# Rows of small factors spread over the partitions: through a scratch row in HBM instead of through TensorE

## The chip, the cores and the metric

The kernel runs on one core of one Trainium2 chip. The metric is the device time of one execution in microseconds (us). The kernel before was timed in three runs; the profile is of one further execution, taken by the hardware profiler.

The core has a matrix engine (TensorE, PE in the profile, with PEld for its weight loads), VectorE (DVE), ScalarE (ACT), GpSimd (POOL) and SyncE (SP). Each engine takes its own instructions in order. DMAs are issued from an engine's queue (here SP's for nearly all loads, POOL's for the ones that add to what is already there) and are moved by 16 DMA engines that all queues share. Work on different engines is ordered by semaphores. SBUF is the memory of 128 partitions that the engines work from, PSUM the one that TensorE writes, HBM the large one outside.

## The reference, cut to what matters

One layer of a decoder trunk, 512 tokens, 1024 channels, in float32:

```python
h = rmsnorm(x, norm1_g) * (1 + scale1) + shift1
qa, ka, va, qd, kd, vd, ga, gd = split(h @ w_in)
out_a = sliding_window_attention(qa, ka, va, sinks)
out_d = differential_attention(qd, kd, vd, lam)              # 4 heads of 128 channels
out_d = rmsnorm(out_d, subln_g) * (1 - lam_init)             # per head
merged = sigmoid(ga) * (out_a @ w_branch_swa) + sigmoid(gd) * (out_d @ w_branch_diff)
x = x + gate1 * (merged @ w_out)
h2 = rmsnorm(x, norm2_g) * (1 + scale2) + shift2
x = x + gate2 * conv_ffn(h2)                                 # up, conv, GELU * gate, down
return rmsnorm(x, final_g)
```

`shift`, `scale` and `gate` come from a small vector `c` by `silu(c) @ w_ada + b_ada`. Two kinds of small factors matter here. The norm of each differential head needs one reciprocal root per token (512 per head). `gate1` and `gate2` are one factor per channel (1024 each).

## The kernel before, in words

Products of two float32 matrices are made of three matmuls of parts (`mm3`, L107 to 110): each operand is split into a rounded high part (a cast on ScalarE) and the remainder (a subtraction on VectorE, `split`, L104).

The order of TensorE's work is written out by hand. The attention part is a list of score, transposition and value steps, with `fill(n)` between them: a fill takes n ticks, and in each tick one step (three matmuls) of a unit is done. Units are the projections that are left: of queries and keys (`add_q`, `add_head`), the two gates' projections with the branches' (`add_gate_a`, `add_gate_d`, `add_merge`). A unit's weights are loaded and split up to two units ahead; `recent` holds the last two subtractions of such splits. `after(n, fn)` calls `fn` n ticks later. VectorE's, ScalarE's and POOL's orders are in most stretches set by a planner, which takes what is ready by priority; `tc.high_priority` and `tc.issue_after` steer it.

Where the change is:

- **The heads' norm.** `diff_values(h)` (L705 to 736) multiplies the probabilities and the values of head h into a bank of PSUM, in which tokens lie along the row and the head's 128 channels over the partitions. ScalarE writes the squares `sq` and the scaled values `of`. After STAT_LAG ticks `stats` sums the squares by four small matmuls (L723), which leaves one sum per token, with the tokens over the partitions: a tile of 128 x 4. The root `rs` (tile `drs`) is made of it on VectorE and POOL (L134 to 151, the power on POOL at L141). But `of` has its tokens along the row, so each root is needed in all partitions of a column. `spread`, NORM_LAG ticks later, does that on TensorE: it broadcasts a column of `rs` to 128 x 128 and transposes it against the identity (L730), four times, into a bank of PSUM `rb`. VectorE multiplies `of` by it (L731), and the result is split into `vv`, the branch's operand in `add_merge`.
- **The gates.** The 32 columns of `late_mod` are filled by VectorE, one per load of a piece of `w_ada` (`ada_rows`, L754). Columns 0 to 7 are `gate1` (`g1c`), 24 to 31 `gate2` (`g2c`), with channels over the partitions. The weights of the output projection are multiplied by `gate1` along their rows (`load_rows`, L987), and the results of the down projection by `gate2` (L1613 and what calls it), so each needs all 1024 factors in every partition. `spread_rows` (L904) does it in two halves of four transpositions (L901) and a copy by ScalarE (L902): for `gate1` 12 ticks after its unit list begins (G1_AT), for `gate2` right before the output projection.
- **The first softmax of the sliding-window part** (L800 to 805): the softmax of head pair 0, then the remainders of two blocks of values (`keep_v(6, (1,))` and two more, L449) and of the second query tile (`stack(..., high=False)`, L426). `turn_va` transposes values into the bank that `keep_v(6, ...)` reads, so it has to wait for it (L486).

Of the kernel before, what the change touches and what calls it, by code (L numbers as in the profile page):

```python
# [8 lines left out]
F32 = mybir.dt.float32  # L9
# [5 lines left out]
P = 128  # L15
D = 1024
S = 512
KT = D // P
NT = S // P
# [6 lines left out]
DIFF_HEADS = 4  # L26
WB = 3
HP = 100000
ST = 6
ADA_LATE = 180  # L30
ADA_EVERY = 5
G1_AT = 12
STAT_LAG = 10
NORM_LAG = 16
VA_AT = 5
SWA_FILL = (2, 1, 6, 2, 2, 2, 2, 3)
DIFF_FILL = (3, 2, 4, 2)
# [6 lines left out]
def kernel(  # L44
# [19 lines left out]
    nc = tc.nc  # L64
# [3 lines left out]
    def pool(name, bufs=1, space=None, stack=ctx):  # L68
        kw = {} if space is None else {"space": space}
        return stack.enter_context(tc.tile_pool(name=name, bufs=bufs, reuse_waits="tile", **kw))  # L70

    cpool = pool("const")
    big = pool("big")
    wp = pool("w")
    ps = pool("ps", space=PSUM)

    def bank(tag, bufs, shape, name, dt=F32):
        return ps.tile(shape, dt, tag=tag, bufs=bufs, name=name)

    def fbank(name):  # L80
        return bank("f", 2, [P, S], name)

    def sbank(name, shape=(P, S)):
        return bank("s", 3, list(shape), name)

    def tbank(name, shape=(P, S)):
        return bank("t", 2, list(shape), name)

    def vbank(name):
        return bank("v", 1, [P, S], name)  # L90

    def raw_tile(shape, name):
        return wp.tile(shape, F32, tag="raw", bufs=4, name=name)

    casts, lows, recent = [None], [None], [None, None]

# [7 lines left out]
    def split(hi, lo, src):  # L104
        return nc.scalar.copy(hi, src), nc.vector.tensor_sub(lo, src, hi.bitcast(F32))

    def mm3(o, lh, ll, rh, rl, start, stop):  # L107
        nc.tensor.matmul(o, lh, rh, start=start, stop=False)  # L108
        nc.tensor.matmul(o, lh, rl, start=False, stop=False)  # L109
        nc.tensor.matmul(o, ll, rh, start=False, stop=stop)  # L110


    ident = cpool.tile([P, P], F32, name="ident")
# [53 lines left out]
    def rstd_m2(dst, ssq, n, d, wpool, plus=None):  # L167
        rstd_end(dst, *rstd_start(ssq, n, d, wpool, plus), n, wpool)
# [41 lines left out]
    acc = [sbank("aka"), sbank("aqa0"), sbank("aqa1"), fbank("av0"), fbank("av1"), vbank("ava"), tbank("av2"), tbank("av3")]  # L210
# [10 lines left out]
    qsc = cpool.tile([P, 4], F32, name="qsc")  # L221
# [153 lines left out]
    for k in range(KT):  # L375
        n = k + 1
# [24 lines left out]
    ap = pool("att", stack=at)  # L401
    qa = big.tile([P, 4, 2, S], F32R, tag="qa", name="qa")
# [15 lines left out]
    def stack(dst, src, scale, soon=True, high=True, low=True):  # L418
        with tc.high_priority(offset=HP) if soon else ExitStack():
            sc = [scale if isinstance(scale, float) else scale[own] for own, _ in halves]  # L420
            for j in range(2) if high else ():
                own = halves[j][0]
                nc.scalar.activation(dst[own, j], src[own], AF.Copy, scale=sc[j])
            for j in range(2) if low else ():
                own, other = halves[j]
                nc.vector.scalar_tensor_tensor(  # L426
                    dst[other, j], src[own], sc[j], dst[own, j].bitcast(F32), ALU.mult, ALU.subtract
                )
# [13 lines left out]
    def keep_v(i, parts=(0, 1)):  # L442
        t = TOKENS[i] * P
        hi, lo = (v[:, :, t : t + P] for v in vv)
        src = acc[i].rearrange("p (h d) -> p h d", d=P)
        if 0 in parts:
            nc.scalar.copy(hi, src)
        if 1 in parts:
            nc.vector.tensor_sub(lo, src, hi.bitcast(F32))  # L449
# [33 lines left out]
    def turn_va():  # L483
        pv = tbank("pva")
        for t in range(NT):
            nc.tensor.transpose(pv[:, t * P : (t + 1) * P], vaT[:, t * P : (t + 1) * P], ident)  # L486
        nc.scalar.copy(va.rearrange("p t d -> p (t d)"), pv)
# [42 lines left out]
    def after(n, fn):  # L530
        later.append([n, fn])
# [40 lines left out]
    def swa_softmax(i):  # L572
        with tc.high_priority(offset=HP):
            c = pairs[i]
            for j in range(2):
                h = i + 4 * j
                slope = 2.0 ** -(h + 1)
                nc.vector.tensor_scalar(c.nm[:, j], c.mx[:, j], -slope, nsink[:, h : h + 1], ALU.mult, ALU.min)
                nc.scalar.activation(c.es[:, j], c.nm[:, j], AF.Exp, bias=sink[:, h : h + 1])
                for n in range(NT):  # L580
                    w = P if n == 0 else 2 * P
                    nc.scalar.activation(
                        c.sb[n][:, j, :w], c.sb[n][:, j, :w], AF.Exp, bias=c.nm[:, j, n : n + 1], scale=slope,
                        accum_out=c.lsum[:, j, n : n + 1],
                    )
                nc.vector.tensor_add(c.lsum[:, j], c.lsum[:, j], c.es[:, j])
                nc.vector.reciprocal(c.lsum[:, j], c.lsum[:, j])
                for n in range(NT):
                    w = P if n == 0 else 2 * P
                    c.end = nc.vector.tensor_scalar_mul(c.sb[n][:, j, :w], c.sb[n][:, j, :w], c.lsum[:, j, n : n + 1])  # L590
# [114 lines left out]
    def diff_values(h):  # L705
        aTh, aTl = aTs[h]
        o = vbank(f"od{h}")
        for k in range(NT):
            q0 = k * P
            mm3(  # L710
                o[:, q0:], vv[0][:, h, k * P : (k + 1) * P], vv[1][:, h, k * P : (k + 1) * P],
                aTh[:, k * AW + q0 : k * AW + 512], aTl[:, k * AW + q0 : k * AW + 512],
                k == 0, k == NT - 1,
            )
        sq = big.tile([P, S], F32, tag="sq2", name=f"sq{h}")
        of = big.tile([P, S], F32, tag=("kvA", "kvB")[h % 2], name=f"of{h}")
        nc.scalar.activation(sq, o, AF.Square)
        nc.scalar.activation(of, o, AF.Copy, scale=sublnc)

        def stats():  # L720
            pss = tbank(f"pss{h}", (P, NT))
            for n in range(NT):
                nc.tensor.matmul(pss[:, n : n + 1], sq[:, n * P : (n + 1) * P], ones[:, 0:1], start=True, stop=True)  # L723
            rs = ap.tile([P, NT], F32, tag="drs", bufs=2, name=f"drs{h}")
            rstd_m2(rs, pss, NT, P, ap)

            def spread():
                rb = tbank(f"rb{h}")
                for n in range(NT):
                    nc.tensor.transpose(rb[:, n * P : (n + 1) * P], rs[:, n : n + 1].to_broadcast([P, P]), ident)  # L730
                nc.vector.tensor_mul(of, of, rb)  # L731
                split(vv[0][:, h], vv[1][:, h], of)

            after(NORM_LAG, spread)

        after(STAT_LAG, stats)


# [55 lines left out]
    with tc.issue_after(vat_copy.ins):  # L794
        fill(SWA_FILL[0])
        swa_scores(0, 0)
        with tc.issue_after(pairs[0].last.ins):
            fill(SWA_FILL[1])
            swa_scores(0, 2)
    with tc.issue_after(pairs[0].last.ins), tc.issue_after(vat_copy.ins):  # L800
        swa_softmax(0)
        keep_v(6, (1,))
        stack(qa[:, 1], acc[2], qsc[:, 1:2], high=False)
        keep_v(4, (1,))
        keep_v(7, (1,))

        lp = cpool.tile([P, 2, 64], F32, name="lp")
        ls = cpool.tile([P, 2], F32, name="ls")
        nlam = cpool.tile([P, 1], F32, name="nlam")
        nc.vector.tensor_mul(lp, lamv[:, 0:4:2], lamv[:, 1:4:2])  # L810
        nc.vector.reduce_sum(ls, lp, axis=mybir.AxisListType.X)
        nc.scalar.activation(ls, ls, AF.Exp)
        nc.vector.tensor_sub(nlam, ls[:, 1:2], ls[:, 0:1])
        nc.vector.tensor_scalar_add(nlam, nlam, -LAM_INIT)
        fill(VA_AT)
        turn_va()
        fill(SWA_FILL[2] - VA_AT)
# [28 lines left out]
    for s in range(4 * DIFF_HEADS):  # L846
        h, n = divmod(s, NT)
# [45 lines left out]
    g1b = gpart(4, [P, D], "g1b")  # L893
    g1c, s2c, a2c, g2c = (late_mod[:, 8 * i : 8 * i + 8] for i in range(4))
    nc.vector.tensor_add(g1c, g1c, blate[:, 0:8])
    nc.vector.tensor_scalar_mul(g1c, g1c, 0.5)

    def spread_half(dst, src, name, hf):
        pr = tbank(f"{name}{hf}")
        for k in range(4):  # L900
            nc.tensor.transpose(pr[:, k * P : (k + 1) * P], src[:, 4 * hf + k : 4 * hf + k + 1].to_broadcast([P, P]), ident)  # L901
        nc.scalar.copy(dst[:, hf * S : (hf + 1) * S], pr)  # L902

    def spread_rows(dst, src, name):  # L904
        for hf in range(2):
            spread_half(dst, src, name, hf)

    after(G1_AT, lambda: spread_rows(g1b, g1c, "pg1"))

    def add_gate_d(j):  # L910
        def gate(wts):
# [54 lines left out]
    nc.vector.scalar_tensor_tensor(a2c, a2c, 1.0, n2g, ALU.add, ALU.mult)  # L966
    nc.vector.tensor_scalar_mul(a2c, a2c, -0.5)
    g2row = big.tile([P, D], F32, tag="row", name="g2row")
    spread_rows(g2row, g2c, "pg2")
    g2b = [g2row[:, hf * S : (hf + 1) * S] for hf in range(2)]  # L970

    x1 = big.tile([P, NT, D], F32, tag="qa", name="x1")
# [318 lines left out]
    last = range(KT - TAIL, KT)  # L1291
# [541 lines left out]
```

## Time and profile before

| | us |
|---|---|
| median of 3 runs | 680.72 |
| lowest and highest run | 680.48, 680.81 |
| the profiled execution, its own time | 680.29 |
| its span in the profile | 678.4 |
| TensorE busy | 669.2 |
| VectorE busy | 569.2 |
| ScalarE busy | 402.2 |
| POOL busy | 66.0 |

Times in the profile count from the start of its span. The attention part runs from about 54 to 242 us, the merge of the branches to 296, the output projection and the norm to 350, the up-projection to 566, the down projection to the end. In the profile, a chain is the work that ended last, followed backwards; a piece of it is the time that a group of instructions adds to the end. In rows of instructions come start, duration, engine, line, operation, what is written and read, and the shape; in rows of groups the count, then the shortest, median and longest duration in ns, and the first and last start in us.

### The profile page before, as it was taken

The page shows a single profiled execution, that of the slowest core. Times are in us where ns is not written, and L with a number is a line of the kernel's source. Part 1 is how long each engine was busy: PE and PEld are TensorE (multiplying, and loading weights), DVE is VectorE, ACT ScalarE, POOL GpSimd, SP SyncE. Part 2 cuts the span into 40 slices and gives each one's busy share as a digit, 9 for nine tenths or more (in the row PEclk, how much of TensorE's full clock was granted, in tenths as well). Part 3 has the DMA queues.
Part 4 walks back from the last instruction along what each step waited for, and adds up shares of the span by engine and source line. Part 5 has one row for each costly group of instructions (what it writes and reads, how often), then busy time and mean ns, then how long its engine had stood idle before and what let it go on. Part 6 is the DMA issues. An engine that isn't in the chain of part 4 may idle for free.

```text
span 678.4 us, 10826 instructions
## 1 busy us (share of the span) xinstructions
PE 669.2 (99%) x4047; PEld 594.8 (88%) x4047; DVE 569.2 (84%) x1054; ACT 402.2 (59%) x702; POOL 66.0 (10%) x74
## 2 busy tenths in 40 slices
PE   8999999999999999999999999999999999999995
PEld 8888887888888888888899999999999998888885
DVE  6988987788887488973689998888888999979997
ACT  6678778565654233342597656565556566656665
POOL 2000000001000000000020120011111003440300
PEclk9999999999999999999999999999999999999999
DMA  9962131444354289767374988887876658996903
GB/s 357 418 227 65 63 125 63 138 143 154 82 168 156 93 291 309 262 173 244 116 126 109 224 211 202 195 201 167 216 172 182 144 187 193 196 205 189 165 0 125
DMA packets 71077, 119.68 MB, mean 176 GB/s; under 512 B 3952, under 2 KB 47728, under 8 KB 71024
## 3 DMA queue, kind: packets, MB, share of 16 engines
q1 hardware_dynamic: 52960, 95.04, 41.6%
q0 software_dynamic: 17776, 23.60, 21.5%
q8 instruction: 32, 0.52, 0.3%
q10 hardware_dynamic: 288, 0.34, 0.2%
q14 instruction: 21, 0.17, 0.1%
HBM read 116.87 MB, written 2.10 MB: 175 GB/s over the span
## 4 chain that ended last, share of the span: by engine, by line
PE 97%; DVE 1%; DMA 1%; ACT 0%; issue 0%; ACTq 0%
PE up L1159 33%; PE dc L1762 15%; PE av L351 3%; PE pga L108 2%; PE pga L110 2%; PE pga L109 2%; PE pgd L110 2%; PE oc L1215 2%; PE pgd L108 2%; PE oc L1216 2%; PE oc L1219 2%; PE pgd L109 2%; PE aqa L348 2%; PE sd L659 2%; PE pq L108 1%; PE pk L108 1%
## 5 line engine op out<-in xcount | busy, mean ns | idle before, releaser
L1159 PE MATMUL up<-t,m_whi 128*128 128x256 f32 x512 | 93.2, 283 | 0.0
L1159 PEld LDWEIGHTS up<-t,m_whi 128*128 128x128 f32 x512 | 79.9, 192 | 0.0
L1159 PE MATMUL up<-t,m_wlo 128*128 128x256 f32 x256 | 72.5, 284 | 0.0
L1159 PE MATMUL up<-bl,p_whi 128*128 128x256 f32 x232 | 65.8, 284 | 0.0
L1159 PE MATMUL up<-bh,p_wlo 128*128 128x256 f32 x232 | 65.8, 284 | 0.0
L1159 PE MATMUL up<-bh,p_whi 128*128 128x256 f32 x232 | 65.8, 284 | 0.0
L1159 PEld LDWEIGHTS up<-t,m_wlo 128*128 128x128 f32 x256 | 49.2, 192 | 0.0
L1159 PEld LDWEIGHTS up<-bh,p_wlo 128*128 128x128 f32 x232 | 44.6, 192 | 0.0
L1159 PEld LDWEIGHTS up<-bh,p_whi 128*128 128x128 f32 x232 | 44.6, 192 | 0.0
L1159 PEld LDWEIGHTS up<-bl,p_whi 128*128 128x128 f32 x232 | 44.6, 192 | 0.0
L1062 POOL DMA_DIRECT2D s<-in_w_up_dram x21 | 27.0, 1365 | 158.2 <-DMA s<-in_w_up_dram 116.8
L1090 ACT CAST m_whi<-s 128x1024 fp32r<-128x1024 f32 x31 | 32.4, 1046 | 15.7 <-DVE s L1084 9.1
L754 DVE CUSTOM_DVE_ANT_0 ra<-ra,csb 128x1024 f32<-128x1024 f32 x32 | 38.7, 1221 | 1.0 <-DMA ra<-in_w_ada_t_dram 1.0
L1094 DVE TENSOR_TENSOR m_wlo<-s,m_whi 128x1024 fp32r<-128x1024 f32 x31 | 37.9, 1221 | 1.3 <-ACT m_whi L1090 1.3
L1159 PE MATMUL up<-t,p_whi 128*128 128x256 f32 x176 | 32.2, 284 | 0.0
L684 ACT ACTIVATE sd<-sd,dmx 128x128 f32<-128x128 f32 (+3 forms) x32 | 17.8, 557 | 21.4 <-DVE dmx L682 17.1
L1159 PEld LDWEIGHTS up<-t,p_whi 128*128 128x128 f32 x176 | 27.5, 192 | 0.1
L1090 ACT CAST p_whi<-wa 128x1024 fp32r<-128x1024 f32 x18 | 18.8, 1042 | 12.6 <-PE up L1159 10.8
L141 POOL TENSOR_TENSOR r<-ms,mhalf 128x4 f32<-128x4 f32 x4 | 5.3, 1322 | 213.7 <-DVE ms L137 213.7
L1166 ACT ACTIVATE gT<-a,cols 128x512 f32<-128x512 f32 x22 | 17.6, 812 | 13.4 <-DVE a L1201 13.0
L1094 DVE TENSOR_TENSOR p_wlo<-wa,p_whi 128x1024 fp32r<-128x1024 f32 x18 | 22.0, 1224 | 4.0 <-ACT p_whi L1090 3.8
L1159 PE MATMUL up<-t,p_wlo 128*128 128x256 f32 x88 | 24.9, 283 | 0.0
(530 smaller groups left out, 2057.8 us busy)
## 6 DMA issues: line engine op xcount, KB each, us to landing
ra<-in_w_ada_t_dram SPq DMA_DIRECT2D x32, 512.0 KB, 4.0
wa<-in_w_up_dram SPq DMA_DIRECT2D x22, 512.0 KB, 4.1
s<-in_w_up_dram SPq DMA_DIRECT2D x21, 512.0 KB, 4.7
s<-in_w_up_dram POOLq DMA_DIRECT2D x21, 512.0 KB, 6.9
adaw<-in_w_ada_t_dram SPq DMA_DIRECT2D x15, 512.0 KB, 9.9
a<-in_w_up_dram SPq DMA_DIRECT2D x11, 512.0 KB, 4.9
b<-in_w_down_dram SPq DMA_DIRECT2D x10, 512.0 KB, 3.7
w<-in_w_first_dram SPq DMA_DIRECT2D x8, 512.0 KB, 9.9
```

The costliest lines, as they stand in the source:

```text
L108: nc.tensor.matmul(o, lh, rh, start=start, stop=False)
L109: nc.tensor.matmul(o, lh, rl, start=False, stop=False)
L110: nc.tensor.matmul(o, ll, rh, start=False, stop=stop)
L351: nc.tensor.matmul(acc[i], ht[:, t : t + P], wts[k][w][:, S:], start=start, stop=stop)
L684: nc.scalar.activation(pm[m], pm[m], AF.Exp, bias=mx[:, m : m + 1], scale=slope, accum_out=lsum[:, m : m + 1])
L754: nc.vector.tensor_tensor_reduce(r, r, csb, 1.0, 0.0, ALU.mult, ALU.add, late_mod[:, idx : idx + 1])
L1062: nc.gpsimd.dma_start(dst, upblock(*blk), accum_op=ALU.add)
L1090: nc.scalar.copy(W[J, name][0], R[J, SRC[name]])
L1094: nc.vector.tensor_sub(lo, R[J, SRC[name]], hi.bitcast(F32))
L1159: nc.tensor.matmul(o[u], w[:, k, cu], b[:, k], start=name in ("p1", "m5", "p2") and k == 0 and x == 0, stop=k == 3 and x == 2, skip_group_ ...
L1166: nc.scalar.activation(grow(j), av[J][:, u], AF.Identity, bias=cv[:, 66 + j : 67 + j], scale=cv[:, 44 + j : 45 + j])
L1762: nc.tensor.matmul((bank2[u] if o is None else o)[:, sl], a[:, q, cu], b[:, q, sl], start=first_mm and x == 0, stop=last_mm and x == 2, sk ...
```

## The change

`spread`'s and `spread_rows`' transpositions go. A new helper `to_rows` writes the small tile to a scratch row in HBM, in the order in which the factors are wanted, and reads that row back into all 128 partitions. Both DMAs are issued from POOL's queue, the second after the first has landed. The heads' rows land in a tile of SBUF instead of a bank of PSUM; the last head's takes the place of `sq`. The store is started right behind the root, in `stats`. STAT_LAG goes from 10 to 6 and NORM_LAG from 16 to 20, so that the product of `of` keeps its tick, and this product is now placed behind the subtractions in `recent`. The gates' rows are started as soon as the program reaches them. Besides, `keep_v(6, (1,))` gets high priority and stands ahead of the first softmax, and the `stack` behind it loses its own.

```diff
-G1_AT = 12
-STAT_LAG = 10
-NORM_LAG = 16
+STAT_LAG = 6
+NORM_LAG = 20
...
+    dp = pool("rows", space=bass.MemoryType.DRAM)
...
+    def to_rows(dst, src, n, name):
+        d = dp.tile([n, P], F32, name=name)
+        nc.gpsimd.dma_start(d.rearrange("k q -> q k"), src)
+        nc.gpsimd.dma_start(dst, d.rearrange("k q -> (k q)").partition_broadcast(P))
...
             rs = ap.tile([P, NT], F32, tag="drs", bufs=2, name=f"drs{h}")
             rstd_m2(rs, pss, NT, P, ap)
 
+            last = h == DIFF_HEADS - 1
+            rb = big.tile([P, S], F32, tag="sq2", name="rb3") if last else ap.tile([P, S], F32, tag="rb", name=f"rb{h}")
+            to_rows(rb, rs, NT, f"rs{h}")
+
             def spread():
-                rb = tbank(f"rb{h}")
-                for n in range(NT):
-                    nc.tensor.transpose(rb[:, n * P : (n + 1) * P], rs[:, n : n + 1].to_broadcast([P, P]), ident)
-                nc.vector.tensor_mul(of, of, rb)
+                with ExitStack() as place:
+                    for b in recent:
+                        place.enter_context(tc.issue_after(b.ins))
+                    nc.vector.tensor_mul(of, of, rb)
                 split(vv[0][:, h], vv[1][:, h], of)
...
     with tc.issue_after(pairs[0].last.ins), tc.issue_after(vat_copy.ins):
+        with tc.high_priority(offset=HP):
+            keep_v(6, (1,))
         swa_softmax(0)
-        keep_v(6, (1,))
-        stack(qa[:, 1], acc[2], qsc[:, 1:2], high=False)
+        stack(qa[:, 1], acc[2], qsc[:, 1:2], soon=False, high=False)
...
-    def spread_half(dst, src, name, hf):
-        pr = tbank(f"{name}{hf}")
-        for k in range(4):
-            nc.tensor.transpose(pr[:, k * P : (k + 1) * P], src[:, 4 * hf + k : 4 * hf + k + 1].to_broadcast([P, P]), ident)
-        nc.scalar.copy(dst[:, hf * S : (hf + 1) * S], pr)
-
-    def spread_rows(dst, src, name):
-        for hf in range(2):
-            spread_half(dst, src, name, hf)
-
-    after(G1_AT, lambda: spread_rows(g1b, g1c, "pg1"))
+    to_rows(g1b, g1c, KT, "g1")
...
-    spread_rows(g2row, g2c, "pg2")
+    to_rows(g2row, g2c, KT, "g2")
```

## The prediction

> **What bounds the kernel now.** I read the page's busy line and its chain first, then the table by stretch, then who waited for whom on TensorE.
>
> ```profile
> span 678.4 us, 10826 instructions
> PE 669.2 (99%) x4047; PEld 594.8 (88%) x4047; DVE 569.2 (84%) x1054; ACT 402.2 (59%) x702; POOL 66.0 (10%) x74
> PE 97%; DVE 1%; DMA 1%; ACT 0%; issue 0%; ACTq 0%
> ```
>
> ```profile
> 68.00:150.00 82.00, 82.00 (x464) 67.37 (x463) 67.21 (x215) 57.91 (x145) 0.00 (x0) 1.00 0.33 110
> 150.00:242.00 92.00, 92.00 (x467) 77.64 (x467) 69.18 (x171) 45.73 (x88) 5.29 (x4) 1.00 0.42 133
> 242.00:296.00 54.00, 54.00 (x240) 44.74 (x239) 47.16 (x65) 18.36 (x24) 1.49 (x1) 1.00 0.85 271
> 350.00:566.00 216.00, 216.00 (x1801) 215.92 (x1800) 193.36 (x272) 133.71 (x200) 24.87 (x20) 1.00 0.74 181
> ```
>
> ```profile
> PE ava L219 <- POOL ones L116: 1.1, 1, 1.1
> PE av L351 <- ACT hThA L337: 0.5, 1, 0.5
> PE pva L486 <- DVE vvl L449: 0.4, 1, 0.4
> ```
>
> The columns of the middle table are stretch, length, then busy time of PE, PEld, DVE, ACT and POOL, granted clock, DMA share and GB/s. From 68 to 566 us PE has no gap in any stretch, at full clock, and the chain is 97% PE. The waits list has only three PE waits, two of them in the start, which is not touched, and the third at L486, which is. So a microsecond of PE work taken out is a microsecond off the end, as long as nothing else becomes late. POOL, which gets the new work, is busy for 0, 5.3 and 1.5 us of the three stretches up to 296 us.
>
> **The change part by part. The transpositions.** Out go sixteen 128x128 transpositions of the heads' roots (L730, four for each of four heads) and sixteen for the two gates (L901, eight each). Their price is read in the chain, where a piece is what the group adds to PE's time:
>
> ```profile
> 166.03 0.44 PE rb L730 x4
> 190.83 0.44 PE rb L730 x4
> 215.96 0.44 PE rb L730 x4
> 233.70 0.44 PE rb L730 x4
> 238.25 0.87 PE pg L901 x8
> 296.29 0.87 PE pg L901 x8
> 67.80 0.23 PE pqa L109
> ```
>
> All of it is on the path: 4 x 0.44 + 2 x 0.87 = 3.50 us. That is 0.11 us each: matmuls overlap, so the chain's piece is the price and not the duration of one instruction. The four ACT copies of L902 go as well; ACT is busy 59%, so that is worth nothing. The product L731 stays, and reads SBUF in place of PSUM; I cost that at nothing.
>
> **The start of the sliding-window part.** `keep_v(6, (1,))`, one DVE subtraction at L449, moves ahead of the first softmax, and the two subtractions of L426 lose their precedence.
>
> ```profile
> 64.15 1.51 DVE L426 SCALAR_TENSOR_TENSOR qa<-aqa,qsc,qa 64x512 fp32r<-64x512 f32 x2
> 65.96 1.29 DVE L449 TENSOR_TENSOR vvl<-av,vvh 128x512 fp32r<-128x512 f32 x2
> 65.98 0.39 PE L110 MATMUL pqa<-hThB,wqa_l 128*128 128x512 f32 x1
> 68.10 1.09 PE L562 MATMUL sw<-ka,qa 128*128 128x128 f32 x8
> 69.77 1.07 DVE L590 TENSOR_SCALAR st<-st,lsum 128x128 f32<-128x128 f32 x4
> ```
>
> Today L426 goes first, then L449, and for the first of its two subtractions PE stands. From the end of the matmul at 65.98 (66.37) to the end of the second matmul after the group (67.80 in the last row of the fence before: its piece begins there) 1.43 us pass; four transpositions and one matmul take 0.44 + 0.23 = 0.67 in the chain. So the wait costs 0.76 us with the refilling of PE's pipeline. With L449 first, at 64.0 to 64.7, it is gone. Next late is L426, which the scores at 68.10 (67.3 then) need: its 1.51 us fit into the time in which DVE waits for ScalarE's exponentials, 65.0 to 66.5. If instead they come behind the whole softmax, they end at 69.77 + 1.07 + 1.51 = 72.35, and PE loses 4.25 us. Bounds: -0.76 to +3.5 us; I take -0.76, since DVE has a hole there to fill.
>
> **The new DMAs.** Each `to_rows` is two DMAs on POOL's queue, twelve in all: a store of 2 KB (heads) or 4 KB (gates) in pieces of 4 bytes, and, behind its landing, a read of 256 or 512 KB spread over the partitions. The trace has no 4-byte store. The rows around it, each for its group of DMAs (fastest, median, slowest from issue to landing): the weight loads that POOL issues (L1062), the final gain spread over the partitions (fgbr, the form of the gates' second DMA), and the stores of the output:
>
> ```profile
> DMA to landing us min/median/max: 5.9/6.6/12.1
> ```
>
> ```profile
> DMA to landing us min/median/max: 7.7/7.7/7.7
> ```
>
> ```profile
> DMA to landing us min/median/max: 2.3/2.6/2.8
> ```
>
> ```profile
> L1062 POOL DMA_DIRECT2D s<-in_w_up_dram x21: 1274/1283/2411, 340.6 to 524.8; - x21
> ```
>
> A pair thus takes between 2 x 2.3 = 4.6 and 2 x 12.1 = 24.2 us; by the nearest rows 6.6 + 7.7 = 14.3, and both rows move twice the bytes or more, under a fuller DMA. I take 10 to 13 us. POOL itself is held some 1.3 us per issue, and stands at the second one until the first has landed. Behind it in the queue wait the next head's power (L141), 20 us later, and the one weight load that POOL issues before 296 us, which is for the up-projection, from about 350 us on. Nobody else.
>
> The gates have time to spare: the gain of the first is finished at 168.1 and first read at 279.4; the second at 279.5 and 617.0.
>
> ```profile
> L896 DVE TENSOR_SCALAR late_mod<-late_mod x1: 170/170/170, 167.9 to 167.9; 128x8 f32<-128x8 f32 x1
> L987 DVE TENSOR_TENSOR wo<-wo,g1b x8: 1220/1222/1228, 279.4 to 310.0; 128x1024 f32<-128x1024 f32 x8
> L965 DVE TENSOR_TENSOR late_mod<-late_mod,cols x1: 176/176/176, 279.3 to 279.3; 128x24 f32<-128x24 f32 x1
> L1629 DVE TENSOR_TENSOR pairs<-chain_kvB,g2row x2: 687/688/689, 617.0 to 617.6; 128x512 f32<-128x512 f32 x2
> ```
>
> So these two pairs cost nothing, even at 24.2 us.
>
> **The heads.** STAT_LAG 10 to 6 moves L723 four ticks earlier, a tick being three matmuls of 0.23 us: 2.7 us. The product L731 keeps its tick (26) and is now put behind the last two weight splits. PE doesn't wait for the product, but DVE takes its work in order: if the rows have not landed, DVE stands, and what is behind it is late. Head 1 is the tightest:
>
> ```profile
> 187.29 0.15 DVE L151 SCALAR_TENSOR_TENSOR drs<-rt,r 128x4 f32<-128x4 f32 x1
> 190.28 1.20 DVE L105 TENSOR_TENSOR wga_l<-wga,wga_h 128x1024 fp32r<-128x1024 f32 x1
> 191.47 0.68 DVE L731 TENSOR_TENSOR of<-of,rb 128x512 f32<-128x512 f32 x1
> 192.53 0.47 DVE L690 SCALAR_TENSOR_TENSOR sd<-sd,dls,sd 128x256 f32<-128x256 f32 x1
> 199.36 0.39 PE L700 MATMUL td<-ident,sd 128*128 128x128 f32 x2
> ```
>
> The root is there at 187.44 - 2.7 = 184.7, the product's turn comes at 191.47, behind the split at 190.28. Behind it stands L690, ending at 193.0, which PE's transposition needs at 199.36: 6.4 us of slack. So PE is free of waits while the pair takes less than 191.5 + 6.4 - 184.7 = 13.2 us. At 14.3 it loses 1.1 us. The root of head 3 has more room:
>
> ```profile
> 224.44 0.17 DVE L151 SCALAR_TENSOR_TENSOR drs<-rt,r 128x4 f32<-128x4 f32 x1
> 235.25 1.22 DVE L105 TENSOR_TENSOR wbd<-wbd,wbd 128x1024 fp32r<-128x1024 f32 x1
> 243.77 0.39 PE L108 MATMUL pB<-vvh,wbd 128*128 128x512 f32 x1
> ```
>
> Its rows land at 224.6 - 2.7 + 14.3 = 236.2, the product's turn is behind the split that ends at 236.5, and PE wants the result at 243.8 (242.5 without the transpositions in between). No cost.
>
> On the store a rule of the Trainium skill speaks against the change: in "DMA: Bandwidth & Descriptors", Rules for kernel authors, a strided last dimension becomes one descriptor per element, and should be made contiguous. No run here shows it yet. What it would do is rival 1 below.
>
> **Sum:** 680.29 (the profiled execution: span 678.4 and 1.9 around it) - 3.50 - 0.76 = 676.03. The median of the runs, 680.72, is 0.43 above the profiled one, so I forecast 676.03 + 0.43 = 676.5.
>
> **The rivals.** (1) The store goes element by element, and head 1 is a little late. The queues' rows price a packet:
>
> ```profile
> q1 hardware_dynamic: 52960, 95.04, 41.6%
> q0 software_dynamic: 17776, 23.60, 21.5%
> ```
>
> 0.215 x 16 x 678.4 / 17776 = 131 ns on POOL's queue, 85 on the other. A head's 512 elements, 32 to an engine, at 131 ns are 4.2 us on top of 2.3: 6.5, and with 7.7 a pair of 14.2 us; as 128 packets of a partition's row it would be 3.4 and 11.1. For it: nothing in the layout lets neighbours go together. Against: those 131 ns are for packets of a kilobyte and more. Time: 676.5 + 1.1 = 677.6. By the skill's rule above this is the case to expect, unless its packets are cheaper than the row.
>
> (2) On the other side: head 1's rows are much later, because the store competes with weight loads (the slowest row of POOL's loads, 12.1). A pair of 12.1 + 7.7 = 19.8 us makes DVE stand 13.0 us at L731 and PE lose 6.6: 676.5 + 6.6 = 683.1. It decides against the change from a pair of 17.5 us on, where the loss is 4.3. Against: DMA is busy 42% in that stretch. If DVE's order puts the root later than now, the point comes sooner.
>
> (3) The gain is given back at the start: L426 behind the softmax, PE loses 4.25 us, 680.7, no change. Against: the hole in DVE's order.
>
> That the transpositions weren't on the path at all is ruled out by the stretches with PE 100% busy.
>
> **How the numbers follow.** Forecast 676.5 (no new wait, 675.7 to 677.2): 0.58. Rival 1, 677.6 (677.2 to 679.3): 0.20. Rival 3, about 680.7: 0.09. Rival 2, 683.1 and more: 0.13. A measurement of this kernel can tell about 0.2%, 1.36 us, from no change: faster is below 679.4, slower above 682.1. Faster 0.78, same 0.09, slower 0.13. The range takes the first three: 675.7 (0.8 us below the forecast, for the spread of the runs and for small shifts of DVE's order) to 680.8.
>
> **What would show it.** No matmul of L730 or L901 in the new profile, and PE's busy time some 3.5 us shorter. PE's wait at L486 gone, and none at the scores of 67.3. DVE idle before the product of head 1 by less than 6 us, and no PE wait at L700. The pair from root to rows in 10 to 13 us; the rows of the gates long before their readers. The prediction is wrong if PE waits at L700 or at the second scores, if POOL's issues of the 4-byte store take several us, or if PE's gain at 240 us isn't there any more at 566 us, where the up-projection ends now.

## The result, and the profile after

The changed kernel takes 703.65 us (median of 4 runs, 702.0 to 704.06); the kernel before, run beside it, 680.6 (680.42 to 680.81). The ratio is 1.0334, 95% interval 1.0316 to 1.0352: 23 us slower, where 4 us faster was forecast. The profiled execution took 703.82 us.

The page of the changed kernel: span, busy time of the engines, and the shares of the chain.

```profile
span 702.0 us, 10785 instructions
PE 674.7 (96%) x4015; PEld 595.0 (85%) x4015; DVE 570.0 (81%) x1054; ACT 400.0 (57%) x698; POOL 72.9 (10%) x86
PE 78%; DMA 10%; DVE 6%; ACT 3%; issue 2%; POOL 1%; SPq 0%; POOLq 0%; ACTq 0%; DVEq 0%
```

The 32 transpositions are gone (4047 matmuls to 4015), but PE's busy time has risen by 5.5 us instead of falling by 3.5, and the chain, 97% PE before, now has 10% DMA and 6% DVE in it. The sum closes: PE is 9.0 us busier than 669.2 - 3.5, it is idle for 27.3 us instead of 9.2, and -3.5 + 9.0 + 18.1 = 23.6, the growth of the span. The table by stretch shows where both are (the columns are those of the table in the prediction; the stretch from 296 to 350 us, which that table leaves out, comes first as it was before):

```profile
296.00:350.00 54.00, 54.00 (x283) 46.12 (x282) 34.39 (x61) 28.26 (x51) 4.10 (x4) 1.00 0.61 177
```

```profile
68.00:150.00 82.00, 81.95 (x465) 67.25 (x464) 66.82 (x211) 58.01 (x145) 0.31 (x1) 1.00 0.35 110
150.00:242.00 92.00, 84.06 (x401) 69.19 (x400) 65.26 (x165) 42.77 (x84) 9.99 (x12) 0.96 0.47 120
242.00:296.00 54.00, 49.32 (x204) 39.98 (x203) 35.92 (x53) 14.00 (x18) 1.11 (x2) 0.94 0.80 260
296.00:350.00 54.00, 48.94 (x207) 39.37 (x206) 29.92 (x35) 17.04 (x22) 2.78 (x3) 0.97 0.66 199
350.00:566.00 216.00, 216.00 (x1747) 213.09 (x1746) 192.03 (x285) 134.75 (x214) 27.48 (x23) 1.00 0.74 174
```

Nothing is lost up to 150 us, and nothing after 350. In the three stretches between, where the six pairs of DMAs are, PE has gaps and its granted clock falls below 1. Setting each matmul's start beside that of the same matmul in the kernel before, PE is 0.2 us behind at 177 us, 7.1 at the third head's values (198), 9.2 at 222, 17.0 at the second product of the branches (267), 16.2 at the output projection's first matmul (313) and 23.6 at its end (361); from there it is constant. So there are three large losses, of 7, 8 and 7 us, and one of 2 us between the first and the second. The largest of PE's new waits (engine, tile, line, who was waited for, then us in total, times, longest):

```profile
PE sd L664 <- ACT qk L442: 4.6, 2, 4.3
PE oc L1215 <- DVE tdall L939: 3.0, 2, 1.5
PE pB L114 <- DVE vvl L110: 2.9, 1, 2.9
PE oc L1215 <- ACT tdall L915: 2.0, 1, 2.0
PE pB L113 <- ACT vvh L110: 1.8, 1, 1.8
```

The two at `pB` follow from rows that landed late: they wait for the remainder and the cast of the last head's product. The row at `sd` waits for a cast of keys, which has nothing to do with the change. What stood ahead of that cast is in ScalarE's timeline (start, length, and in brackets the idle time before and who ended it):

```profile
184.82 1.04 ACT L110 CAST wga_h<-wga 128x1024 fp32r<-128x1024 f32 x1 [5.36 <-DMA wga<-in_w_tiles_dram]
185.89 2.11 ACT L442 CAST qk<-qk 64x1024 fp32r<-64x1024 f32 x2
```

ScalarE takes its work in order, and stood 5.36 us at the cast of a gate's weights that had not landed. That load was issued on SP's queue at 176.5 and took 8.2 us; the first gate's store had been issued at 170.6 and landed at 181.1. In the kernel before, the list of DMAs (queue, count, size, median us from issue to landing) has for these weights, and for the output projection's and the branch's, which come next:

```profile
wga<-in_w_tiles_dram SPq DMA_DIRECT2D x8, 512.0 KB, 3.7
...
wo<-in_w_out_dram SPq DMA_DIRECT2D x8, 512.0 KB, 4.0
...
wba<-in_w_branch_swa_dram SPq DMA_DIRECT2D x8, 256.0 KB, 4.0
```

The same happens to others. Some of the pieces of the chain that are DMAs (start, length), and from the list of DMAs of the changed kernel the rows of the new ones:

```profile
184.44 12.05 DMA wba<-in_w_branch_swa_dram
...
234.27 11.10 DMA rs<-drs
245.95 7.22 DMA rb<-rs
300.76 9.15 DMA wo<-in_w_out_dram
```

```profile
rb<-rs POOLq DMA_DIRECT2D x4, 256.0 KB, 7.1
...
rs<-drs POOLq DMA_DIRECT2D x4, 2.0 KB, 10.7
g<-late_mod POOLq DMA_DIRECT2D x2, 4.0 KB, 10.1
```

A store of 2 KB takes 10.7 us and one of 4 KB 10.1 (medians); from the issue of the store to the landing of the rows, the heads' pairs take 17.7 to 21.2 us and the second gate's 14.3. The first gate's read was issued only at 246.5, behind the last head's on POOL's queue, and still came early enough for its reader. Beside the stores stand the losses: the branch's weights took 12 us beside the second head's store (issued 178.7, landed 191.8), the output projection's 9 beside the second gate's (296.9 to 306.6). While the first of these waits, the DMA engines are hardly busy, and then they rush. Three stretches of the changed kernel, granted clock, DMA share and GB/s in the last columns:

```profile
187.00:190.00 3.00, 2.62 (x10) 2.34 (x11) 1.47 (x2) 2.95 (x6) 0.00 (x0) 0.50 0.12 17
190.00:193.00 3.00, 3.00 (x10) 2.35 (x9) 3.00 (x15) 1.01 (x4) 0.56 (x1) 0.60 0.29 14
193.00:198.00 5.00, 5.00 (x26) 4.12 (x25) 2.28 (x8) 1.95 (x7) 0.00 (x0) 1.00 0.96 299
```

Two loads of 256 KB had been issued at 183.8 and 184.4; at 14 to 17 GB/s they don't move, at 299 GB/s they land. The clock column tells where the 9.0 us of longer matmuls come from: by the table above, 0.04 x 92 + 0.06 x 54 + 0.03 x 54 = 8.5 us of full clock are missing, an estimate from rounded shares. After PE's wait of 4.25 us before 187.0 the granted clock is 0.50, then 0.60, and 1.00 again from 193. By the Trainium skill, "TensorE: Matmul & The Clock Gate", What's actually happening, the clock goes to half after an idle window of about 3.4 us; these rows agree.

The change's own readers, VectorE's products, stand at the first and third heads for 1.3 and 2.8 us, at the second not at all, and at the last for 11:

```profile
253.19 0.69 DVE L740 TENSOR_TENSOR of<-of,rb 128x512 f32<-128x512 f32 x1 [10.99 <-DMA rb<-rs]
```

So by PE's waits the second loss comes from rows that landed late, and the first and the third from weights that landed late.

**The theories.** A: the transposing store of 4-byte pieces takes 10 us and, for as long as it runs, whatever load is in flight beside it stands; in-order engines pass that on to PE. B: the edit at the start has changed the planner's orders. C: the rows are late for their readers, and that is all. D: the spreading reads of 256 and 512 KB take the bandwidth. E: POOL's queue, with two DMAs one behind the other, holds up what comes after.

### The profile page after: what moved, and what is told of

It is laid out like the page before. It is cut to its first block, busy times and chain, and to the rows that moved or that the text cites. A ratio compares the mean times of both kernels' runs of the same rounds, so it can differ in the third digit from the quotient of the medians.

```text
span 702.0 us, 10785 instructions
## 1 busy us (share of the span) xinstructions
PE 674.7 (96%) x4015; PEld 595.0 (85%) x4015; DVE 570.0 (81%) x1054; ACT 400.0 (57%) x698; POOL 72.9 (10%) x86
## 3 DMA queue, kind: packets, MB, share of 16 engines
q0 software_dynamic: 18576, 25.71, 21.8%
## 4 chain that ended last, share of the span: by engine, by line
PE 78%; DMA 10%; DVE 6%; ACT 3%; issue 2%; POOL 1%; SPq 0%; POOLq 0%; ACTq 0%; DVEq 0%
PE up L1159 32%; PE dc L1762 15%; PE av L356 3%; DMA rs<-drs 3%; PE oc L1215 2%; DMA rb<-rs 2%; PE oc L1216 2%; PE oc L1219 2%; DMA wo<-in_w_out_dram 2%; DMA wba<-in_w_branch_swa_dram 2%; PE aqa L353 2%; PE pgd L114 1%; PE pgd L113 1%; PE pgd L115 1%; PE pk L113 1%
## 5 line engine op out<-in xcount | busy, mean ns | idle before, releaser
L1090 ACT CAST m_whi<-s 128x1024 fp32r<-128x1024 f32 x31 | 32.5, 1047 | 15.7 <-DVE s L1084 9.1
L763 DVE CUSTOM_DVE_ANT_0 ra<-ra,csb 128x1024 f32<-128x1024 f32 x32 | 38.7, 1220 | 2.7 <-DMA ra<-in_w_ada_t_dram 2.6
L689 ACT ACTIVATE sd<-sd,dmx 128x128 f32<-128x128 f32 (+3 forms) x32 | 17.8, 557 | 20.5 <-DVE dmx L687 16.3
L1084 DVE TENSOR_TENSOR s<-s,wa 128x1024 f32<-128x1024 f32 x20 | 24.3, 1217 | 0.1
```

Of the source, the lines that this page charges most:

```text
L689: nc.scalar.activation(pm[m], pm[m], AF.Exp, bias=mx[:, m : m + 1], scale=slope, accum_out=lsum[:, m : m + 1])
L763: nc.vector.tensor_tensor_reduce(r, r, csb, 1.0, 0.0, ALU.mult, ALU.add, late_mod[:, idx : idx + 1])
L1084: nc.vector.tensor_add(src, src, R[J, "a11" if name == "m6" else "a12"])
L1090: nc.scalar.copy(W[J, name][0], R[J, SRC[name]])
```

## The experiments

**Each part alone.** First the edit of the first softmax, in the kernel before:

```diff
+        with tc.high_priority(offset=HP):
+            keep_v(6, (1,))
         swa_softmax(0)
-        keep_v(6, (1,))
-        stack(qa[:, 1], acc[2], qsc[:, 1:2], high=False)
+        stack(qa[:, 1], acc[2], qsc[:, 1:2], soon=False, high=False)
```

> The kernel before with the edit of the first softmax alone (the remainder of block 6 first, at high priority; the second query tile without its precedence). Theory A (the 4-byte stores hold the DMA engines and cost all of the time lost): the edit is worth next to nothing either way, 679.8 to 681.2, because in the changed kernel TensorE had gained 0.7 us at the transposition of the values but stood 0.1 us behind the kernel before from the second scores on. Rival B (the edit changes the planner's orders of VectorE and ScalarE for all that follows, and that makes the operands of the heads late): 685 or more. The prediction's step: 679.9.

Measured: 680.72 us against 680.58, ratio 1.0002 (0.9993 to 1.0011). B falls. PE gained 0.6 us at the transposition of the values, as in the changed kernel, and by the second scores at 74 us nothing of it was left: it gave back 0.4 us at the next matmul, in front of which it now waits 0.3 us for the remainders at L449, and the rest at the transpositions behind 71 us.

The heads' part alone (`to_rows` for the four roots, both lags, the product's place; gates and start as before):

> The kernel before with the heads' part of the change alone (rows of the roots through the scratch row, the lags of 6 and 20 ticks, the product behind the last two splits); the gates' transpositions and the start stay as before. Theory A: the losses at the second-last score block (about 4.5 to 7 us) and at the last head's product (about 8 us) stay, the one in the output projection (7.4 us) goes with the second gate's store: 680.6 - 1.75 + 7 to 9 + 8 = 694 to 696. Rival C (row lateness at the heads is everything and the rest follows): 703 or more. Rival F (the gates' pairs make the losses): 679 to 681.

Measured: 700.29 us, ratio 1.0289 (1.0274 to 1.0304), 20 us slower. That is above the 694 to 696 that A gave. PE is 7.4 us behind at 203 us, 15.7 at the second product of the branches, and 20.5 at the end of the output projection, where there is no second gate's store: it waits 2.8 us there for a bank that ScalarE empties late. A had left that out; it is the place at which two later versions lose their lead.

The gates' part alone:

```diff
-    after(G1_AT, lambda: spread_rows(g1b, g1c, "pg1"))
+    to_rows(g1b, g1c, KT, "g1")
...
-    spread_rows(g2row, g2c, "pg2")
+    to_rows(g2row, g2c, KT, "g2")
```

> The kernel before with the gates' part of the change alone: both gates' rows by the 4-byte store and the spreading read; heads and start as before. The prediction's step: two pairs cost nothing, so 680.6 - 1.75 = 678.9. Theory A: nobody waits for these rows, but the first store holds the gate weights in flight at 170 us and the second the output projection's at 300 us: TensorE loses 4 to 7.5 us at the scores behind 182 us and 7 to 11 us in the output projection, so 690 to 697. Rival C (only rows that land late cost): 678 to 680.

Measured: 692.4 us against 680.38, ratio 1.0175 (1.016 to 1.0189). Nobody waits for these rows, and still 12 us are lost: PE is 6.3 us behind after the scores behind the first store, and loses 8 more in the output projection behind the second (the two spared groups of transpositions give 1.75 back). C falls as the whole cause.

**The stores alone.** In the kernel before, with all transpositions, six stores that nobody reads, at the change's places:

```diff
+    def to_scratch(src, n, name):
+        d = dp.tile([n, P], F32, name=name)
+        nc.gpsimd.dma_start(d.rearrange("k q -> q k"), src)
...
             rstd_m2(rs, pss, NT, P, ap)
+            to_scratch(rs, NT, f"rs{h}")
```

> The kernel before, whole, with all its transpositions, and six 4-byte stores into scratch rows beside them, at the program places of the change (behind each head's root, behind the first gate, behind the second), which nobody reads. Theory A (the stores hold the DMA engines for about 10 us each, and loads in flight beside them land late): each store takes 10 to 11 us from issue to landing, the gates' weights, the branches' and the output projection's beside them take 8 to 12 us, TensorE waits at two or three places that had no wait, and the time is 690 to 700. Rival C (the time is lost because the rows themselves land late and VectorE stands before the heads' products): nobody waits for these stores, so 680 to 682. Rival D (the reads of 256 to 512 KB that spread the rows take the bandwidth): there are no such reads here, so 680 to 682 too.

Measured: 715.61 us, ratio 1.051 (1.0484 to 1.0536): 35 us, more than the change itself and more than A's 690 to 700. No read, no row that is late, no wait on POOL is left, so none of C, D and E is needed for a loss of this size. The list of DMAs of this kernel, and the loads in its chain:

```profile
rs<-drs POOLq DMA_DIRECT2D x4, 2.0 KB, 10.1
g<-late_mod POOLq DMA_DIRECT2D x2, 4.0 KB, 12.0
```

```profile
174.57 10.68 DMA wga<-in_w_tiles_dram
198.80 11.20 DMA wga<-in_w_tiles_dram
224.82 11.46 DMA wgd<-in_w_tiles_dram
...
307.66 10.83 DMA wo<-in_w_out_dram
```

Four loads of 512 KB take 11 us in place of 4, each issued 3 to 6 us behind a store (POOL issues them at 168.6, 195.0, 222.0 and 303.6). Why this costs more than the change itself wasn't taken apart; that other loads lie behind the stores here than there is a guess.

**The same stores, their pieces apart.** One thing else: every 4-byte piece goes 512 bytes from the next.

```diff
-        d = dp.tile([n, P], F32, name=name)
-        nc.gpsimd.dma_start(d.rearrange("k q -> q k"), src)
+        d = dp.tile([n, P, P], F32, name=name)
+        nc.gpsimd.dma_start(d[:, :, 0].rearrange("k q -> q k"), src)
```

> As the kernel with the dead stores (everything of the kernel before, and six 4-byte stores that nobody reads), with one thing else: every 4-byte piece goes 512 bytes from the next in HBM, not beside it. The same number of pieces, the same bytes, queue, places. Theory G (pieces that share a line of HBM are what is slow, and hold up the loads): stores of 2 to 3 us, loads beside them as ever, 680 to 682. Theory A as first put (the price is by the piece): 715 as with the neighbours.

Measured: 680.49 us against 680.61, ratio 0.9995 (0.9985 to 1.0004). All 35 us are gone, with the same number of pieces, the same bytes, queue and places:

```profile
rs<-drs POOLq DMA_DIRECT2D x4, 2.0 KB, 2.7
g<-late_mod POOLq DMA_DIRECT2D x2, 4.0 KB, 3.9
```

So A was right about the store and the loads, but not about the price by the piece: slow are 4-byte pieces that lie side by side in HBM and come from different partitions.

**The price of one store by itself.** Behind the last output of the kernel before, single DMAs, twice each, with nothing else in flight where no load is named:

```diff
+            d = dp.tile([n, P], F32, name=f"d_turned{n}")
+            q.dma_start(d.rearrange("k q -> q k"), z[:, :n])
...
+            d = dp.tile([P, n], F32, name=f"d_aslies{n}")
+            q.dma_start(d, z[:, :n])
...
+            d = dp.tile([n, P, P], F32, name=f"d_apart{n}")
+            q.dma_start(d[:, :, 0].rearrange("k q -> q k"), z[:, :n])
```

> The kernel before, whole, and behind its last output a ladder of single DMAs, twice, each starting when the one ahead has landed (POOL clears the tiles between them): stores of a 128 x n tile turned (pieces of 4 bytes, neighbours in HBM from neighbouring partitions) for n = 1, 2, 4, 8; the same for n = 4 with every piece 512 bytes from the next; as it lies for n = 4 and 8; turned from SP's queue; a 512 KB weight load alone, beside a turned store and beside one as it lies; the 256 KB spreading read right behind a turned store, and alone. The time means nothing; the durations do. Theory A (the price is by the piece, and it holds the DMA engines for whatever comes behind): turned n = 4 takes 9 to 11 us and n = 8 no less; as it lies under 3 us; n = 1 under 4; the queue makes no difference; the load takes 3 to 4 us alone and beside the store as it lies, 8 to 12 beside the turned one. Rival G (neighbouring pieces in the same line of HBM are what is slow): the pieces 512 bytes apart take under 4 us. Rival H (POOL's software queue is slow at making descriptors): from SP's queue the turned store takes under 4 us, and the load beside POOL's is not held up. The spreading read behind the turned store: 7 us by the changed kernel's rows; if it is 4 us here, then the 7 us there were loads caught up behind the store.

The list of DMAs of this kernel (queue, count, size, median us from issue to landing):

```profile
x<-d_turned POOLq DMA_DIRECT2D x2, 256.0 KB, 4.6
x<-d_aslies POOLq DMA_DIRECT2D x2, 256.0 KB, 3.4
...
d_turned<-x POOLq DMA_DIRECT2D x4, 2.0 KB, 9.6
d_turned<-x POOLq DMA_DIRECT2D x2, 4.0 KB, 9.2
d_turned<-x POOLq DMA_DIRECT2D x2, 1.0 KB, 8.8
d_turned<-x POOLq DMA_DIRECT2D x2, 0.5 KB, 8.1
d_apart<-x POOLq DMA_DIRECT2D x2, 2.0 KB, 2.2
d_aslies<-x POOLq DMA_DIRECT2D x2, 4.0 KB, 1.7
d_turned<-x SPq DMA_DIRECT2D x2, 2.0 KB, 8.9
```

The row of 9.6 mixes two stores by themselves (8.9 and 9.2) with two that had the 512 KB load beside them (10.0 and 10.5). Turned, 128 pieces take 8.1 us, 512 about 9.0 and 1024 9.2, so the count is not the price; 512 pieces, each 512 bytes from the next, take 2.2, as G has it; as it lies, 4 KB take 1.7. SP's queue makes no difference (8.9), so H falls, and with it the idea that POOL is to blame for the length of the store; whether a store from SP's queue holds up loads as well was not run. The 512 KB load took 4.3 us alone, about 5 beside the store as it lies, and up to 13.0 beside the turned one: the slowest in the answer for its tile is

```profile
DMA to landing us min/median/max: 4.3/4.8/13.0
```

The spreading read takes 3.4 us by itself and 4.6 right behind a turned store with nothing else in flight. That its 7.1 us in the changed kernel come from the held-up loads, which land at the same time, is inferred from this.

How far apart is enough? Stores of 128 pieces at growing distance, of larger pieces, and of fewer partitions:

```diff
+        d = dp.tile([P, step], F32, name=f"d_step{step}")
+        nc.gpsimd.dma_start(d[:, 0:1], z[:, 0:1])
...
+        d = dp.tile([P, n], F32, name=f"d_piece{n}")
+        nc.gpsimd.dma_start(d, z[:, 0:n])
```

> The kernel before and behind it, one at a time and twice, stores of 128 x 1 values (128 pieces of 4 bytes) with 4, 8, 16, 32, 64, 128, 256 and 512 bytes from one piece to the next; stores of pieces of 8, 16 and 32 bytes side by side; stores of 16, 32 and 64 pieces of 4 bytes side by side. The time means nothing. Theory G (writers of the same line of HBM go one after the other): the time falls in proportion to the pieces in a line: from 8.1 us at 4 bytes to about 5 at 8, 3.3 at 16, 2.5 at 32 and under 2.3 from 64 on; pieces of 8 bytes side by side about 5, of 16 about 2.5; 16 and 32 pieces of 4 bytes: 8 us as well if the line is 64 bytes (several lines go side by side), 2.5 to 3.5 us if it is 512 bytes. Rival (only what is smaller than some piece is slow, however many share a line): a step, not a slope.

POOL's timeline of this kernel; a clearing starts when the store ahead has landed, so a store's time runs from the start of its issue to the start of the next row. The first three are 4, 8 and 16 bytes apart:

```profile
679.33 0.59 POOL L1797 DMA_DIRECT2D d_step<-x  x1 [0.46 <-POOL x L1809]
686.65 0.10 POOL L1809 MEMSET x<- 128x8 f32 x1 [6.73 <-DMA d_step<-x]
687.16 0.55 POOL L1797 DMA_DIRECT2D d_step<-x  x1 [0.34 <-POOL x L1809]
690.71 0.10 POOL L1809 MEMSET x<- 128x8 f32 x1 [3.00 <-DMA d_step<-x]
691.20 0.54 POOL L1797 DMA_DIRECT2D d_step<-x  x1 [0.31 <-POOL x L1809]
692.98 0.10 POOL L1809 MEMSET x<- 128x8 f32 x1 [1.24 <-DMA d_step<-x]
```

7.3, 3.6 and 1.8 us, and 1.8 at every distance from 16 bytes to 512. Pieces of 8 bytes side by side take 3.6 and 3.4, of 16 bytes 1.7 and 2.1. So the time goes with how close the pieces lie, steeper than expected, down to a floor at 16 bytes; a piece of 4 bytes is not slow as such. With fewer pieces side by side it is 1.6 to 2.2 us for 16, 3.5 to 4.5 for 32 and 7.0 for 64, which fits neither line size that the expectation named. What in the memory or the DMA engines does this stays open.

**The change with a store that has no small neighbours.** First the changed kernel with the tile stored as it lies, and the strides moved to the products:

```diff
-        d = dp.tile([n, P], F32, name=name)
-        nc.gpsimd.dma_start(d.rearrange("k q -> q k"), src)
-        nc.gpsimd.dma_start(dst, d.rearrange("k q -> (k q)").partition_broadcast(P))
+        d = dp.tile([P, n], F32, name=name)
+        nc.gpsimd.dma_start(d, src)
+        nc.gpsimd.dma_start(dst, d.rearrange("q k -> (q k)").partition_broadcast(P))
...
-        nc.vector.tensor_mul(r, r, gate)
+        nc.vector.tensor_mul(grid(r), grid(r), by_k(gate, KT))
```

> The changed kernel, whole, with one thing else: the store writes the small tile as it lies (16 or 32 bytes in a row per partition), so the scratch row has the other order, and the products read the rows that landed with a stride. Reads back, queue, places and waits stay. Theory A: a store takes 2.5 to 5 us instead of 10.5, the loads beside it land as before, VectorE's stand before the last head's product goes from 11.0 to under 5 us, and the time is 676 to 681. Rival D (the spreading reads of 256 to 512 KB take the bandwidth): 690 or more, as these are unchanged. Rival E (two DMAs on POOL's queue, the second waiting for the first, hold up what is queued there): 690 or more as well, less some us for the shorter store.

Measured: 685.64 us against 680.58, ratio 1.007 (1.005 to 1.0091): 18 of the 23 us are back, though not to A's 676 to 681. The stores take 1.8 and 3.4 us and the heads' reads 4.2, though the reads and the queue are unchanged, so D and E fall as the cause of the 23 us. At the first matmul of the output projection PE is 2.5 us ahead of the kernel before. Then it loses 5. By the timeline the products with the strided gate have become slow, and VectorE frees PE's banks and asks for the next weights later; this was not tested by itself. VectorE's group of them (1220 ns each in the kernel before):

```profile
L993 DVE TENSOR_TENSOR wo<-wo,g1b 128x1024 f32<-128x1024 f32 x8 | 17.1, 2138 | 8.1 <-DMA wo<-in_w_out_dram 8.1
```

The same store for the heads alone, with the gates transposed:

> As the contiguous store, for the heads alone: store of the roots as they lie, strided reading in the four heads' products, and both gates by transposition as before, start as before. Theory A: what the contiguous store had left (5 us over the kernel before) came from its strided products of the output projection's weights (2.14 us each instead of 1.22), which are not here: 680.6 - 1.75 = 678.9, with the pipeline's spread 678.2 to 680.2. Rival (something in the heads' pairs still costs): 682 or more.

Measured: 680.65 us against 680.38, ratio 1.0007 (0.9998 to 1.0016). That is above the 678.2 to 680.2 expected; the 1.75 us didn't come. PE was 0.5 us ahead at the output projection, and then waited 1.7 us for a bank that ScalarE had not yet emptied.

**A version for both sides.** One small transposition turns the tile on PE (128 x 4 to 4 x 128, six in all instead of 32), and rows of 512 bytes are stored; the start is as before:

```diff
+        pt = tbank(f"pt{name}", (n, P))
+        nc.tensor.transpose(pt, src, ident)
+        s = dst[0:n, 0:P]
+        nc.scalar.copy(s, pt)
         d = dp.tile([n, P], F32, name=name)
-        nc.gpsimd.dma_start(d.rearrange("k q -> q k"), src)
+        nc.gpsimd.dma_start(d, s)
```

> The kernel before with the change's scratch rows, but the small tile is first turned by one transposition on TensorE (128 x 4 or 128 x 8, six in all instead of 32), copied by ScalarE into the tile of the rows, and stored as rows of 512 bytes, 4 or 8 of them; the spreading reads are the change's, the products read without a stride, the start is as before. Ticks from the norm's sums to the turn 9, from there to the product 11. Theory A: stores 2 to 3 us, reads 4 to 5 us, no load held up; six transpositions cost 0.7 of the 3.5 us, so 680.6 - 2.8 = 677.8, with a wait of up to 2 us where the root is late for the turn: 677.5 to 680. It would then be the version faster than both. Rival D (the spreading reads cost): 682 or more.

Measured: 681.54 us against 680.38 (12 runs, 679.82 to 685.54), ratio 1.002 (1.0007 to 1.0033), above the 677.5 to 680 expected. In the profiled execution (680.68 us) PE is 2.67 us ahead at the output projection, and then waits. PE's wait and ScalarE's timeline around it:

```profile
PE oc L1223 <- ACT g2row L101: 2.8, 1, 2.8
```

```profile
300.63 1.04 ACT L116 CAST m5w<-s_t 128x1024 fp32r<-128x1024 f32 x1 [6.42 <-DMA s_t<-in_w_up_dram]
301.58 0.25 ACT L101 COPY g2row<-ptg 8x128 f32<-8x128 f32 x1
```

The copy that empties PE's bank stands behind a cast that waits 6.42 us for a weight of the up-projection. So this copy alone goes to VectorE:

```diff
-    to_rows(g2row, g2c, KT, "g2")
+    to_rows(g2row, g2c, KT, "g2", nc.vector.tensor_copy)
```

> As the rowed version (one small transposition, rows of 512 bytes), with one thing else: the turned tile of the second gate is copied by VectorE, not ScalarE. In the rowed version TensorE stood 2.67 us ahead of the kernel before at the first matmul of the output projection and lost 3.1 us there: ScalarE's copy of the second gate stood behind a cast whose weights landed at 300.6 us, and TensorE waited 2.84 us for the bank. Theory A2 (the gain was 2.7 us and was given back at that one bank): 680.4 - 2.7 = 677.7, 677 to 679, and the lead holds from 296 us to the end. Rival (the weights of the output projection themselves are the next bound, so TensorE waits for the next one): 680 to 681 again, with the wait at another tile between 296 and 337 us.

Measured: 677.5 us against 680.61, ratio 0.9953 (0.994 to 0.9965), the fastest of all; the five runs lie between 677.44 and 677.78. PE's lead is 2.68 us at the start of the output projection and 2.71 at its end, and there is no wait in that stretch:

```profile
296.00:350.00 54.00, 54.00 (x289) 46.51 (x288) 34.91 (x62) 29.47 (x54) 5.23 (x6) 1.00 0.73 196
```

## Why the prediction was wrong

- **The transpositions** were sized rightly: 26 of 32 taken out at 0.11 us are 2.8 us, and the last version's trace keeps 2.7. They lie on the path.
- **"As long as nothing else becomes late"** was the condition, and it already fails by itself at the output projection: two versions lost their whole lead there, at a bank that is emptied in ScalarE's order, and the heads' part alone 4.8 us at the same bank. Only the list of waits of a kernel that arrives earlier shows such a place.
- **The start**: the forecast of -0.76 us was a local truth. VectorE's hole was there, L426 ran in it, and PE gained 0.6 us at the transposition of the values; the next operands were late in turn, and nothing arrived at the end (1.0002).
- **The new DMAs: the step that failed.** The pair's own time was put at 10 to 13 us. The heads' pairs took 17.7 to 21.2, within the bounds of 4.6 to 24.2; the term that was too small is the store, 6.6 us by the nearest row and 10.4 to 13.2 measured. (That both rows move twice the bytes is true for the heads alone; the gates' read is as large as its row.) By the prediction's own working head 1's pair, 21.2 us, costs 8.0 us at head 1's product, where VectorE didn't stand. The larger error was the question asked of the DMAs: who waits for the rows, and who is queued behind on POOL. "Nobody else", and for the gates "cost nothing, even at 24.2 us". The runs showed that loads in flight during the 10 us of the store pay for it, on SP's queue too: the gates' two pairs alone cost 12 us, and stores that nobody reads 35.
- **The heads**: head 1, called the tightest, didn't stand at its product in the changed kernel; head 3, "No cost", stood 10.99 us. Head 1's root came at 178.4 us and not at 184.7, and its product's turn at 201.7, behind the held-up loads, and not at 191.5: both steps of that working had moved.
- **Rival 2** named the conflict between store and loads, and had it the wrong way round: it let the store be slowed by the loads, and priced one place at 6.6 us. There were three places of 7 to 8, and the chance of 0.13 that it gave to "slower" met the result by another way than its own. Rival 1's price of 131 ns a packet had little to multiply: POOL's queue counts 18576 packets in the changed kernel, against 17776 before, and the same 18576 in the last version, whose stores are rows of 512 bytes.
- **The rule of the Trainium skill** ("DMA: Bandwidth & Descriptors", Rules for kernel authors: a strided last dimension becomes one descriptor per element) pointed at the right DMA. Following its advice helped (the store as it lies, the rows of 512 bytes), but it is not needed for the store to be fast: 512 pieces took about 9.0 us side by side and 2.2 us 512 bytes apart, so the count of elements is not the price here. In its Specifications the same page says that transfers under 512 bytes are read-modify-writes; pieces of 4 bytes from 16 bytes apart on are at the floor of 1.8 us all the same.

## What to carry to other kernels

Price a DMA not only by who waits for its data but by what else is in flight while it runs: here a store of 2 KB held up the loads beside it for some 10 us. To turn a small tile on its way to HBM, turn it on the chip first and store whole rows, or keep the pieces at least 16 bytes apart (run here with 128 pieces; 512 and 1024 were run 512 bytes apart). When work leaves the busiest engine, look at the next place where it takes a bank or an operand from an in-order queue with a load ahead: the gain may end there, as it did twice, until one copy was moved to another engine.

## What the hardware showed that was not expected

- A store of 4-byte pieces that lie side by side and come from different partitions took 7.0 us for 64 pieces, 8.1 for 128 and 9.2 for 1024; for 512 it was 8.9 to 9.2 from POOL's queue and 8.9 from SP's. 128 pieces 16 bytes apart took 1.8.
- While such a store ran, a 512 KB load beside it took 13.0 us instead of 4.3; in the changed kernel the DMA engines moved 14 to 17 GB/s at a busy share of 0.12 to 0.29, so a low DMA share was no sign that a load could move.
- A product of VectorE whose second operand is read with a stride of 32 bytes took 2138 ns in place of 1220, and one of half the size with a stride of 16 bytes 1066 in place of 692.
